# The gate projection of a decoder layer: two of its three split products in one wide matmul

## The chip, the cores and the metric

One core of a Trainium2 chip runs the whole layer as one program. The metric is the device time of one execution in microseconds (us). The kernel before took 356.97 us as the median of 3 executions (356.93 to 357.1). The profile comes from one further execution.

## The reference

The reference is one hybrid decoder layer on 256 tokens of width 1024, all in float32. Cut to what matters here:

```
h    = rmsnorm(x)
proj = h @ w_in               # queries, keys, values of two mixers | g_m (2 x 1024 columns)
gm   = sigmoid(g_m)           # the merge gates
mixed = gm[:, :1024] * (y_nsa @ w_up_nsa) + gm[:, 1024:] * (y_moba @ w_up_moba)
x    = x + mixed @ w_out
x    = x + relu(rmsnorm(x) @ w_ff1)**2 @ w_ff2
return rmsnorm(x)
```

`y_nsa` and `y_moba` are the outputs of two attention mixers. The change lies in the projection to `g_m`, the gates.

## The kernel before

**Split products.** TensorE is given its operands as float32r, and the layer is float32. So every operand is split into a high and a low part: ScalarE (ACT) writes the high part with a Copy (`whi`, line 114), and VectorE (DVE) subtracts it from the number to get the low part (`wlo`, line 116). A product is then three matmuls into the same PSUM columns: high weights with high activations, high weights with low activations, low weights with high activations (`mm3`, line 256). The activations of the gates are split in the same way, into `hTh` and `hTl`.

**Chunks and slots.** The weights come in chunks of 128x2048 numbers (`CHUNKS`, line 24). Each chunk has a slot of the program: its matmuls are a list, and `run_slot` (line 227) issues them in order and puts other work of all engines between them at given fractions of the list (`at(0.1, ...)`). Inside one engine everything runs strictly in the order in which it was issued. In the slot of chunk c, the chunk c+2 is split in halves (`split_events`, line 295) and the chunk c+5 is loaded.

**The gates.** Chunks 12 to 19 are the eight gate groups, here called groups 0 to 7. A group makes two blocks of 128 gates x 256 tokens. Each block sums 8 steps of 128 model columns, with three matmuls of 256 columns in a step: 48 matmuls in a group (`two_blocks` and `wstat`, lines 790 and 285). Both blocks of a group share one PSUM bank, except in group 0, which has a bank for each. The banks go round in the order `acc0`, `tp`, `acc1` (line 819; `next_bank`, line 68). At fraction 0.02 of the next slot `gm_evac` (line 808) takes the bank with one ScalarE Tanh of 512 columns (line 816).

**Attention beside the gates.** The same slots hold the attention, two head pairs at a time (`unit_events`, line 657). In an odd slot (groups 1, 3, 5, 7) TensorE makes the scores `Sa`, `Sb` and the products with the values (`yb`), VectorE masks the scores and finds their maxima (lines 572 to 576), and ScalarE takes the exponentials (line 585). In the even slot after it (groups 2, 4, 6 and the first slot after the gates) VectorE normalizes the probabilities (`d_norm`, lines 590 to 599, at fraction 0.1) and TensorE transposes them (`d_trans`, line 615, at fraction 0.78; for the first pair of them at another place). ScalarE and VectorE then copy the transposes to SBUF (lines 617 and 619).

**After the gates.** Two slots each of `upn` and `upm` multiply the mixers' outputs up and merge them with the gates. Four slots `wout` follow, here called output slots 0 to 3, and then the feed-forward part (FF1, FF2). All of them draw banks from the same round until the first FF1 slot, where line 1156 sets the round anew: `turn["acc"] = ["acc1", "acc0"]`, so that its first block always goes into bank `acc1`. The results of an output slot are added to x by VectorE (line 906), scaled and rounded to high parts by ScalarE (line 910), and VectorE makes the low parts (line 913). Output slot 3 has a bank for each of its two blocks; its second block is added at fraction 0.02 of the first FF1 slot.

Of the kernel before, what the change touches and what calls it, by code (L numbers as in the profile page):

```python
# [9 lines left out]
F32R = mybir.dt.float32r  # L10
AF = mybir.ActivationFunctionType
ALU = mybir.AluOpType
# [33 lines left out]
def hybrid_layer(ctx: ExitStack, tc: tile.TileContext, gxd, w, w1c, small, const, gf, out):  # L46
    nc = tc.nc
    act, dve, pool, pe = nc.scalar, nc.vector, nc.gpsimd, nc.tensor
# [3 lines left out]
    cp = ctx.enter_context(tc.tile_pool(name="cp", bufs=1))  # L52
# [15 lines left out]
    def next_bank(kind):  # L68
        t = turn[kind]
        t.append(t.pop(0))  # L70
        return bank(t[-1], kind)

    def acc_tile():
        return next_bank("acc")
# [13 lines left out]
    raw, hi, lo = {}, {}, {}  # L88
# [87 lines left out]

    def act_tiles(name):
        return [cp.tile([128, 2048 + e], F32R, name=name + n, tag="act" + n.upper())  # L180
                for n, e in (("h", 128), ("l", 16))]

    def act_views(tiles, o):
        return (a[:, o:o + 2048].rearrange("p (k q) -> p k q", k=8) for a in tiles)

    h_tiles = act_tiles("hT")
    hTh, hTl = act_views(h_tiles, 16)
    hNh, hNl = act_views(h_tiles, 0)  # L190

    for kt in range(8):
        act.activation(hTh[:, kt, :], xT[:, kt, :], AF.Copy, scale=g1[:, kt:kt + 1])
# [30 lines left out]
    def at(pos, f, *a):  # L224
        ev.append((pos, f, a))

    def run_slot(mms):
        n = len(mms)
        es = sorted(ev, key=lambda e: e[0])
        ev.clear()  # L230
        j = 0
        for i, m in enumerate(mms):
            while j < len(es) and es[j][0] <= i / n:
                es[j][1](*es[j][2])
                j += 1
            m()
        while j < len(es):
            es[j][1](*es[j][2])
            j += 1

    def paired(v):

        return v.rearrange("p (a b) -> p b a", a=2)
# [5 lines left out]
                           a=2, b=128)  # L249

    def mm(o, l, r, start, stop):
        if len(r.shape) > len(o.shape):
            o = o.rearrange("p (b a) -> p b a", a=2)
        pe.matmul(o, l, r, start=start, stop=stop, skip_group_check=True)  # L254

    def mm3(o, lh, ll, rh, rl, first, last):
        return [lambda: mm(o, lh, rh, first, False),
                lambda: mm(o, lh, rl, False, False),
                lambda: mm(o, ll, rh, False, last)]
# [25 lines left out]
    def wstat(o, c, off, nk, ncol, ah, al, ks=None, first=0, last=None):  # L285

        r = []
        last = nk - 1 if last is None else last
        for k in (range(nk) if ks is None else ks):
            a = k * ncol + off  # L290
            r += mm3(o, hi[c][:, a:a + 128], lo[c][:, a:a + 128], paired(ah[:, k, :]),
                     paired(al[:, k, :]), k == first, k == last)
        return r

    def split_events(c, hs, ls):
# [8 lines left out]
    def std_events(c):  # L304
        if c == C_QM + 1:
            split_events(c, (0.0, 0.51), (0.3, 0.52))
        elif c == C_VM + 1:
            split_events(c, (0.0, 0.06), (0.09, 0.6))
        elif 9 <= c < 20 and c % 2:
            split_events(c, (0.0, 0.06), (0.09, 0.46))  # L310
        elif 9 <= c < 20:
            split_events(c, (0.0, 0.45), (0.3, 0.8 if c > 10 else 0.92))
        else:
            split_events(c, (0.0, 0.45), (0.3, 0.46))
# [342 lines left out]
    def unit_events(s):  # L657
        d = (s - 9) // 2
        if not 9 <= s <= 21:
            return  # L660
        if s % 2 == 0:
            at(0.1, d_norm, d)
            if s != 12:
                at(0.78 if d else 0.9, d_trans, d)
            return
        late = {11: 0.04, 13: 0.22}.get(s, 0)
        if s == 13:
            at(0.06, d_trans, d - 1)
        if d > 0:
            at(0.1 + late, d_cmp, d - 1)  # L670
        if d < 6:
            at(0.1 + late, d_scores, d)
        if d > 0:
            at(0.1 + late, d_pv, d - 1)
        if d < 6:
            at(0.11 + late, d_max, d)
            at(0.2 + late if s > 12 else 0.5, d_exp, d, 1)
            at(0.22 + late if s > 12 else 0.52, d_exp, d, 0)
        if d > 0:
            at(0.12 + late, d_yevac, d - 1)  # L680
# [4 lines left out]
    for sec, c0, n in groups:  # L685
# [6 lines left out]
        for i in range(2):  # L692
            c = c0 + i
# [96 lines left out]
    def two_blocks(c, ah, al, late=8, whole=None):  # L790

        if late < 8:
            outs = [acc_tile()[:, 0:256] for _ in range(2)]
            whole = None
            order = [range(late), range(late, 8)]
        else:
            whole = whole or acc_tile()
            outs = [whole[:, 0:256], whole[:, 256:512]]
            order = [range(8)]
        mms = []  # L800
        for ks in order:
            for m in range(2):
                mms += wstat(outs[m], c, m * 128, 8, 256, ah, al, ks=ks, last=7)
        return mms, outs, whole

    sgs = [ap_.tile([128, 8, 256], F32, name="sga", tag="early")]

    def gm_evac(g, outs, whole):
        if g == 4:
            sgs.append(ap_.tile([128, 8, 256], F32, name="sgb", tag="w1"))  # L810
        v = sgs[g // 4][:, 2 * (g % 4):2 * (g % 4) + 2]
        if whole is None:
            for m in range(2):
                act.activation(v[:, m], outs[m], AF.Tanh, scale=0.5)
        else:
            act.activation(v.rearrange("p b q -> p (b q)"), whole, AF.Tanh, scale=0.5)

    prev = [(evac_tm, ("vm", 1, accs[1], 512))]
    turn["acc"] = ["acc0", "tp", "acc1"]
    for g in range(8):  # L820
        c = C_GM + g
        if g == 0:
            for k in (4, 6):
                at(0.0, norm_parts, k, k + 2)
        std_events(c)
        unit_events(c)
        for f, a in prev:
            at(0.02, f, *a)
        mms, outs, whole = two_blocks(c, hNh, hNl, 8 if g else 4)
        run_slot(mms)  # L830
        prev = [(gm_evac, (g, outs, whole))]

    mxh, mxl = act_views(act_tiles("mx"), 0)

    def up_views(k):
        return [v[:, 2 * k:2 * k + 2].rearrange("p b q -> p (b q)")
# [18 lines left out]
    for sec, c0, kind, evac in (("upn", C_UPN, "n", upn_evac), ("upm", C_UPM, "m", upm_evac)):  # L855
        for i in range(2):
            c = c0 + i
            if c == C_UPN:
                split_events(c, (0.3, 0.3), (0.4, 0.4))
            elif c == C_UPM:  # L860
                split_events(c, (0.0, 0.0), (0.1, 0.53))
            elif c < C_UPM:
                split_events(c, (0.0, 0.0), (0.1, 0.1))
            else:
                split_events(c, (0.0, 0.0), (9, 9))
            unit_events(c)
            for f, a in prev:
                at(0.02, f, *a)
                if f == upm_evac:
                    at(0.15, mix_l, a[0])  # L870
            accs = [acc_tile(), acc_tile()]
            mms = []
            for m in range(4):
                mms += wstat(accs[m // 2][:, m % 2 * 256:m % 2 * 256 + 256], c, m * 128, 4, 512,
                             yTh[kind], yTl[kind])
            at(0.52, evac, 2 * i, accs[0])
            if kind == "m":
                at(0.7, mix_l, 2 * i)
            run_slot(mms)
            prev = [(evac, (2 * i + 1, accs[1]))]  # L880
# [50 lines left out]
    for i in range(4):  # L931
        c = C_WOUT + i
        if i == 0:
            at(0.03, mix_l, 3)
            lo_late(0.35, c - 1)
        elif i == 1:
            lo_late(0.03, c - 1)
        split_events(c, (0.0, 0.1) if i else (0.0, 0.3), ((9, 9), (0.3, 0.3), (0.3, 0.3), (9, 9))[i])
        for f, a in prev:
            at(0.02, f, *a)  # L940
        if i == 1:
            at(0.01, open_ff)
            for j in range(4):
                at(0.9, gamma_rows, j)
        if i == 3:
            outs = [acc_tile()[:, 0:256] for _ in range(2)]
            at(0.52, wout_evac, i, outs, (0,))
            run_slot([m for j in range(2)
                      for m in wstat(outs[j], c, j * 128, 8, 256, mxh, mxl)])
            prev = [(wout_evac, (i, outs, (1,)))]  # L950
        else:
            mms, outs, _ = two_blocks(c, mxh, mxl, 6 if i == 0 else 8)
            run_slot(mms)
            prev = [(wout_evac, (i, outs))]
# [191 lines left out]
    for c in range(C_FF, NCH - 2):  # L1146
        sec, i, _ = CHUNKS[c]
# [5 lines left out]
        prev = []  # L1153
        if sec == "ff1":
# [4 lines left out]
            mms, outs, whole = two_blocks(c, FB["h2h"], FB["h2l"], 8 if i else 6)  # L1159
# [4 lines left out]
            prev = [(squares, (i, outs, whole))]  # L1164
# [17 lines left out]
    whole = ops[order[3]]  # L1182
# [148 lines left out]
```

## Time and profile before

| | |
|---|---|
| median of 3 executions | 356.97 us |
| the profiled execution | 357.63 us |
| its span in the trace | 355.9 us |
| TensorE busy | 347.4 us |
| VectorE busy | 312.9 us |
| ScalarE busy | 242.9 us |
| granted TensorE clock, mean | 0.995 |

The span runs from the first to the last instruction in the trace; the profiled execution's own time lies 1.7 us above it. A row of the timeline reads: start and duration in us, engine, line, operation, output and inputs, count, and in square brackets the idle time of the engine ahead of it and what ended that. A row of the chain reads: start, duration, engine, what it writes, line and count. Matmuls are pipelined: a row's duration is a latency, and the distance of starts is the pace.

### The profile page before, as it was taken

The page shows a single profiled execution, that of the slowest core. Times are in us where ns is not written, and L with a number is a line of the kernel's source. Part 1 is how long each engine was busy: PE and PEld are TensorE (multiplying, and loading weights), DVE is VectorE, ACT ScalarE, POOL GpSimd, SP SyncE. Part 2 cuts the span into 40 slices and gives each one's busy share as a digit, 9 for nine tenths or more (in the row PEclk, how much of TensorE's full clock was granted, in tenths as well). Part 3 has the DMA queues.
Part 4 walks back from the last instruction along what each step waited for, and adds up shares of the span by engine and source line. Part 5 has one row for each costly group of instructions (what it writes and reads, how often), then busy time and mean ns, then how long its engine had stood idle before and what let it go on. Part 6 is the DMA issues. An engine that isn't in the chain of part 4 may idle for free.

```text
span 355.9 us, 6587 instructions
## 1 busy us (share of the span) xinstructions
PE 347.4 (98%) x2667; PEld 324.4 (91%) x2667; DVE 312.9 (88%) x456; ACT 242.9 (68%) x367; POOL 25.9 (7%) x46
## 2 busy tenths in 40 slices
PE   7999999999999999999999999999999999999993
PEld 5997888889999999999999999999999999999982
DVE  4988999999876859767968999999999999999794
ACT  5974965879646757625448799877777769676713
POOL 1010000000000000000312011110111111000001
PEclk9999999999999999999999999999999999999997
DMA  7987535434443333633697957888889888774003
GB/s 263 389 335 283 193 120 192 161 120 126 159 174 135 120 120 131 225 120 118 171 330 227 346 163 273 297 260 258 263 281 289 278 268 301 196 308 170 1 2 118
DMA packets 14447, 73.69 MB, mean 207 GB/s; under 512 B 1744, under 2 KB 3152, under 8 KB 7120
## 3 DMA queue, kind: packets, MB, share of 16 engines
q1 hardware_dynamic: 10512, 64.68, 50.4%
q0 software_dynamic: 3328, 7.87, 9.5%
q10 hardware_dynamic: 576, 0.72, 0.6%
q8 instruction: 21, 0.34, 0.4%
q14 instruction: 10, 0.08, 0.1%
HBM read 72.21 MB, written 1.05 MB: 206 GB/s over the span
## 4 chain that ended last, share of the span: by engine, by line
PE 90%; DVE 3%; ACT 2%; DMA 1%; issue 1%; SPq 0%; POOLq 0%; POOL 0%; DVEq 0%
PE acc L254 61%; PE o L254 10%; PE yb L254 5%; PE tp L254 3%; PE kvbacc L254 3%; PE qacc L254 2%; PE Sa L254 2%; PE Sa L615 2%; DMA gx<-in_gx_dram 1%; PE tp L354 1%; PE Sb L615 1%; DVE x L1066 1%; PE Sb L254 1%; PE o L927 0%; ACT whi L114 0%
## 5 line engine op out<-in xcount | busy, mean ns | idle before, releaser
L114 ACT ACTIVATE whi<-raw 128x1024 fp32r<-128x1024 f32 (+3 forms) x82 | 90.1, 1120 | 43.1 <-DMA raw<-in_ff_dram 26.7
L116 DVE TENSOR_TENSOR wlo<-raw,whi 128x1024 fp32r<-128x1024 f32 (+3 forms) x83 | 105.0, 1285 | 5.3 <-ACT whi L114 4.8
L254 PE MATMUL acc<-h2h,whi 128*128 128x256 f32 x256 | 70.5, 275 | 0.0
L254 PE MATMUL acc<-h2h,wlo 128*128 128x256 f32 x256 | 70.4, 275 | 0.0
L254 PE MATMUL acc<-h2l,whi 128*128 128x256 f32 x256 | 70.4, 275 | 0.0
L254 PEld LDWEIGHTS acc<-h2l,whi 128*128 128x128 f32 x256 | 49.2, 192 | 0.0
L254 PEld LDWEIGHTS acc<-h2h,wlo 128*128 128x128 f32 x256 | 49.2, 192 | 0.0
L254 PEld LDWEIGHTS acc<-h2h,whi 128*128 128x128 f32 x256 | 49.2, 192 | 0.0
L254 PE MATMUL acc<-hTh,wlo 128*128 128x256 f32 x128 | 35.8, 279 | 0.0
L254 PE MATMUL acc<-hTl,whi 128*128 128x256 f32 x128 | 35.4, 277 | 0.0
L254 PE MATMUL acc<-hTh,whi 128*128 128x256 f32 x128 | 35.3, 276 | 0.0
L1037 ACT ACTIVATE whi<-wt 128x2048 fp32r<-128x2048 f32 x14 | 26.7, 1907 | 9.4 <-PE acc L254 7.4
L1039 DVE TENSOR_TENSOR wlo<-wt,whi 128x2048 fp32r<-128x2048 f32 x14 | 32.0, 2284 | 0.2
L254 PEld LDWEIGHTS acc<-hTh,wlo 128*128 128x128 f32 x128 | 24.5, 192 | 0.5 <-issue 0.5
L254 PEld LDWEIGHTS acc<-hTl,whi 128*128 128x128 f32 x128 | 24.6, 192 | 0.2 <-issue 0.2
L254 PE MATMUL acc<-whi,hTh 128*128 128x512 f32 (+2 forms) x65 | 24.1, 371 | 0.5 <-ACT whi L114 0.4
L254 PEld LDWEIGHTS acc<-hTh,whi 128*128 128x128 f32 x128 | 24.6, 192 | 0.0
L1030 DVE TENSOR_TENSOR sl<-raw,sh 128x1536 fp32r<-128x1536 f32 x14 | 24.5, 1748 | 0.0
L254 PE MATMUL acc<-wlo,hTh 128*128 128x512 f32 (+2 forms) x65 | 24.1, 371 | 0.3 <-DVE wlo L116 0.2
L254 PE MATMUL acc<-whi,hTl 128*128 128x512 f32 (+2 forms) x65 | 23.8, 366 | 0.0
L1028 ACT ACTIVATE sh<-raw 128x1536 fp32r<-128x1536 f32 x14 | 20.8, 1488 | 0.0
L1021 POOL DMA_DIRECT2D wt<-in_ff_dram x14 | 12.3, 880 | 89.5 <-DMA wt<-in_ff_dram 89.5
(322 smaller groups left out, 891.1 us busy)
## 6 DMA issues: line engine op xcount, KB each, us to landing
raw<-in_ff_dram SPq DMA_DIRECT2D x32, 1024.0 KB, 7.7
raw<-in_gm_dram SPq DMA_DIRECT2D x8, 1024.0 KB, 4.8
wt<-in_ff_dram POOLq DMA_DIRECT2D x28, 256.0 KB, 7.4
raw<-in_wout_dram SPq DMA_DIRECT2D x4, 1024.0 KB, 4.8
raw<-in_q_dram SPq DMA_DIRECT2D x2, 1024.0 KB, 6.7
raw<-in_qm_dram SPq DMA_DIRECT2D x2, 1024.0 KB, 6.4
raw<-in_km_dram SPq DMA_DIRECT2D x2, 1024.0 KB, 5.6
raw<-in_vm_dram SPq DMA_DIRECT2D x2, 1024.0 KB, 4.8
```

The costliest lines, as they stand in the source:

```text
L114: act.activation(hi[c][:, a:b], raw[c][:, a:b], AF.Copy)
L116: dve.tensor_tensor(lo[c][:, a:b], raw[c][:, a:b], hi[c][:, a:b].bitcast(F32), op=ALU.subtract)
L254: pe.matmul(o, l, r, start=start, stop=stop, skip_group_check=True)
L354: pe.transpose(tp[:, j * 256 + t * 128:j * 256 + t * 128 + 128], src[:, t, (2 * i + j) * 128:(2 * i + j + 1) * 128], ident)
L615: pe.transpose(T[:, j, x, o:o + 128], P[:, 2 * x + j, c:c + 128], ident)
L1021: pool.dma_start(T[:, 1], w["ff2"][i, :, 0:512], accum_op=ALU.add)
L1028: act.activation(singles[c][0], v, AF.Copy)
L1030: dve.tensor_tensor(singles[c][1], v, singles[c][0].bitcast(F32), op=ALU.subtract)
L1037: act.activation(hi[c], v, AF.Copy)
L1039: dve.tensor_tensor(lo[c], v, hi[c].bitcast(F32), op=ALU.subtract)
L1066: dve.scalar_tensor_tensor(x1[:, t, s], y, fst[:, 4 + t:5 + t], x1[:, t, s], op0=ALU.mult, op1=ALU.add)
```

## The change

High and low activations are now one tile `hT` of 2 x 8 x 256 numbers, so that one matmul can read both: `wstat2` multiplies the high weights with the high and the low activations of a step in one product of 512 columns. It writes two halves of a whole bank: columns 0 to 255 hold high x high, columns 256 to 511 high x low. The low weights with the high activations add to the first half with a matmul of 256 columns. A step has two matmuls where it had three, and a group 32 where it had 48.

So each block needs a bank of its own, and the two halves are still to be added: `gm_sum` copies the second half to SBUF on ScalarE and VectorE adds the first half from PSUM to it; `gm_tanh` is a further ScalarE instruction on the sum. Of a group's first block the sum stands at fraction 0.52 of its own slot, of the second block at 0.02 of the next slot, and the Tanh half a slot later than the sum. The diff, cut to its core:

```
-        return [cp.tile([128, 2048 + e], F32R, name=name + n, tag="act" + n.upper())
-                for n, e in (("h", 128), ("l", 16))]
+        return cp.tile([128, 2, 8, 256], F32R, name=name, tag="act")
...
+    def wstat2(o, c, off, nk, ncol, a, ks=None):
+        r = []
+        for k in (range(nk) if ks is None else ks):
+            w = slice(k * ncol + off, k * ncol + off + 128)
+            both = a[:, :, k, :].rearrange("p x (a b) -> p x b a", a=2)
+            m = [lambda w=w, both=both, k=k: mm(o, hi[c][:, w], both, k == 0, k == nk - 1),
+                 lambda w=w, k=k: mm(o[:, 0:256], lo[c][:, w], paired(a[:, 0, k, :]), False, False)]
+            r += m if k < nk - 1 else m[::-1]
+        return r
...
-            act.activation(v.rearrange("p b q -> p (b q)"), whole, AF.Tanh, scale=0.5)
+        act.activation(gate(g, m), o[:, 256:512], AF.Copy)
+        dve.tensor_tensor(gate(g, m), o[:, 0:256], gate(g, m), op=ALU.add)
+
+    def gm_tanh(g, m):
+        act.activation(gate(g, m), gate(g, m), AF.Tanh, scale=0.5)
...
-        mms, outs, whole = two_blocks(c, hNh, hNl, 8 if g else 4)
-        run_slot(mms)
-        prev = [(gm_evac, (g, outs, whole))]
+        if g == 1:
+            at(0.53, gm_tanh, 0, 0)
+        if g:
+            at(0.53, gm_tanh, g - 1, 1)
+        outs = [acc_tile() for _ in range(2)]
+        prev = [(gm_sum, (g, 1, outs[1]))]
+        if g:
+            at(0.52, gm_sum, g, 0, outs[0])
+            prev.append((gm_tanh, (g, 0)))
+        else:
+            prev = [(gm_sum, (g, 0, outs[0]))] + prev
+        run_slot([f for ks in ([range(8)] if g else [range(4), range(4, 8)]) for m in range(2)
+                  for f in wstat2(outs[m], c, m * 128, 8, 256, hT, ks)])
+    prev.append((gm_tanh, (7, 1)))
```

The gates drew 9 banks from the round before (two in group 0, then one a group) and draw 16 now. 9 is a multiple of the three banks and 16 is not: every later slot gets the bank that stands one place further. In output slot 3 the two blocks had `acc0` and `tp` before and have `tp` and `acc1` now.

On VectorE, this is the order before around the end of group 3 and the start of group 4. Lines 572 to 576 are the mask and maxima of group 3's scores, line 116 writes low weights, and lines 590 to 599 are the normalizing in group 4's slot:

```order
L572 TENSOR_TENSOR Sa<-Sa,kc 128x4x128
L575 TENSOR_REDUCE ust<-Sa 128x2x2
L576 TENSOR_SCALAR ust<-ust 128x4
L572 TENSOR_TENSOR Sb<-Sb,kc 128x2x256
L575 TENSOR_REDUCE ust<-Sb 128x2x2
L576 TENSOR_SCALAR ust<-ust 128x4
L655 TENSOR_TENSOR yTln<-yb,yThn 128x256
L116 TENSOR_TENSOR wlo<-raw,whi 128x1024
L590 TENSOR_SCALAR ust<-ust 128x8
L591 RECIPROCAL ust<-ust 128x8
```

The same place now (the lines have moved by 10; line 825 is the new sum):

```order
L116 TENSOR_TENSOR wlo<-raw,whi 128x1024
L825 TENSOR_TENSOR sga<-acc,sga 128x256
L116 TENSOR_TENSOR wlo<-raw,whi 128x1024
L582 TENSOR_TENSOR Sa<-Sa,kc 128x4x128
L585 TENSOR_REDUCE ust<-Sa 128x2x2
L586 TENSOR_SCALAR ust<-ust 128x4
L582 TENSOR_TENSOR Sb<-Sb,kc 128x2x256
L585 TENSOR_REDUCE ust<-Sb 128x2x2
L586 TENSOR_SCALAR ust<-ust 128x4
L665 TENSOR_TENSOR yTln<-yb,yThn 128x256
L116 TENSOR_TENSOR wlo<-raw,whi 128x1024
L825 TENSOR_TENSOR sga<-acc,sga 128x256 x2
```

Two sums, of both blocks of group 3, stand ahead of the normalizing, and the sum of group 2's second block stands ahead of the low weights at the top and so of the mask of group 3's scores.

On ScalarE, before, from the exponentials of group 3 to the copy of group 4's transposes:

```order
L585 ACTIVATE P,ust<-Sa,ust 128x256 x4
L585 ACTIVATE P,ust<-Sb,ust 128x128 x4
L114 ACTIVATE whi<-raw 128x1024
L816 ACTIVATE sga<-acc 128x512
L114 ACTIVATE whi<-raw 128x1024
L617 ACTIVATE PT<-Sa 128x2x2x256
```

and now (line 824 copies a half bank, line 828 is the Tanh):

```order
L595 ACTIVATE P,ust<-Sa,ust 128x256 x4
L595 ACTIVATE P,ust<-Sb,ust 128x128 x4
L824 ACTIVATE sga<-acc 128x256
L828 ACTIVATE sga<-sga 128x256
L114 ACTIVATE whi<-raw 128x1024
L824 ACTIVATE sga<-acc 128x256
L828 ACTIVATE sga<-sga 128x256
L114 ACTIVATE whi<-raw 128x1024
L824 ACTIVATE sgb<-acc 128x256
L828 ACTIVATE sga<-sga 128x256
L627 ACTIVATE PT<-Sa 128x2x2x256
```

The copy for the second sum stands behind the first copy, a Tanh and half a chunk of high weights.

On TensorE, the last products of output slot 3 and the first of the first FF1 slot, before (the numbers tell tiles apart: `acc_2209` is the second block of output slot 3, `acc_2280` the first of FF1):

```order
L254 MATMUL acc_2209<-mxh_1713,whi_2059 128x256
L254 MATMUL acc_2209<-mxl_1714,whi_2059 128x256
L254 MATMUL acc_2209<-mxh_1713,wlo_2060 128x256
L254 MATMUL acc_2280<-h2h_2072,whi_2146 128x256 [waits PE_49,DVE_49,Activation_49,Pool_49]
L254 MATMUL acc_2280<-h2l_2073,whi_2146 128x256
```

and now (`acc_2125` is the second block of output slot 3, `acc_2196` the first of FF1):

```order
L252 MATMUL acc_2125<-mx_1627,wlo_1976 128x256
L252 MATMUL acc_2125<-mx_1627,whi_1975 128x256 x2
L252 MATMUL acc_2125<-mx_1627,wlo_1976 128x256
L252 MATMUL acc_2196<-h2h_1988,whi_2062 128x256 [waits DVE_49,Activation_49,Pool_49]
L252 MATMUL acc_2196<-h2l_1989,whi_2062 128x256
```

The matmuls are the same; what the wait on VectorE counts to is another instruction. `acc_2280` took bank `acc1`, which output slot 2 had used last, and its wait ends with the adds of output slot 2. `acc_2196` takes bank `acc1` too, which now holds the block before it, `acc_2125`, and its wait ends with the add of that block.

More of the change, by code (lines that the diff above doesn't have):

```diff
@@ L172, in hybrid_layer, with act_tile @@
     cmpm = kc_[:, K_CMP:K_CMP + 30].rearrange("p (t i) -> p t i", t=2)
-    def act_tiles(name):
-        return [cp.tile([128, 2048 + e], F32R, name=name + n, tag="act" + n.upper())
-                for n, e in (("h", 128), ("l", 16))]
[L183 to L190, printed above, removed]
+    def act_tile(name):
+        return cp.tile([128, 2, 8, 256], F32R, name=name, tag="act")
+    hT = act_tile("hT")
+    hTh, hTl = hT[:, 0], hT[:, 1]
+    hNh, hNl = hTh, hTl
     for kt in range(8):
@@ L251, in mm @@
     def mm(o, l, r, start, stop):
-        if len(r.shape) > len(o.shape):
+        if len(r.shape) == 4:
+            o = o.rearrange("p (x b a) -> p x b a", x=2, a=2)
+        elif len(r.shape) > len(o.shape):
             o = o.rearrange("p (b a) -> p b a", a=2)
@@ L806, in hybrid_layer, with gate, gm_sum @@
     sgs = [ap_.tile([128, 8, 256], F32, name="sga", tag="early")]
-    def gm_evac(g, outs, whole):
-        if g == 4:
+    def gate(g, m):
+        return sgs[g // 4][:, 2 * (g % 4) + m]
+    def gm_sum(g, m, o):
+        if g == 4 and m == 0:
             sgs.append(ap_.tile([128, 8, 256], F32, name="sgb", tag="w1"))
[L811 to L816, printed above, removed]
+        act.activation(gate(g, m), o[:, 256:512], AF.Copy)
+        dve.tensor_tensor(gate(g, m), o[:, 0:256], gate(g, m), op=ALU.add)
+    def gm_tanh(g, m):
+        act.activation(gate(g, m), gate(g, m), AF.Tanh, scale=0.5)
     prev = [(evac_tm, ("vm", 1, accs[1], 512))]
@@ L828, in hybrid_layer @@
             at(0.02, f, *a)
-        mms, outs, whole = two_blocks(c, hNh, hNl, 8 if g else 4)
-        run_slot(mms)
-        prev = [(gm_evac, (g, outs, whole))]
-    mxh, mxl = act_views(act_tiles("mx"), 0)
+        if g == 1:
[12 more added lines that the diff above has]
+    prev.append((gm_tanh, (7, 1)))
+    mx = act_tile("mx")
+    mxh, mxl = mx[:, 0], mx[:, 1]
     def up_views(k):
```

## The prediction

> **What bounds the kernel now.** I read the page first, for the shares of the engines and of the chain:
>
> ```profile
> PE 347.4 (98%) x2667; PEld 324.4 (91%) x2667; DVE 312.9 (88%) x456; ACT 242.9 (68%) x367; POOL 25.9 (7%) x46
> PE 90%; DVE 3%; ACT 2%; DMA 1%; issue 1%; SPq 0%; POOLq 0%; POOL 0%; DVEq 0%
> ```
>
> TensorE is busy for 98% of the span. A saving shows only if it shortens TensorE's own stream, and a wait of TensorE anywhere is lost in full. VectorE (88%) is close behind and can be late. Then I read the chain of waits in order of time (start, us, engine, what, line, count):
>
> ```profile
> 91.72 8.01 PE acc L254 x70
> 99.73 0.87 PE Sa L615 x8
> ...
> 105.77 9.24 PE acc L254 x81
> 115.01 0.87 PE Sa L615 x8
> ...
> 121.34 9.24 PE acc L254 x81
> 130.58 0.87 PE Sa L615 x8
> ...
> 210.32 5.36 PE acc L254 x48
> 215.68 2.59 PE o L254 x12
> ```
>
> From 91.7 us on the chain is TensorE without a break: the gates, then the transposes of groups 2, 4 and 6 (line 615), and so on to the end of FF2. The last two rows give the paces. 48 products of 256 columns take 5.36 us, 111.7 ns each; 12 of 512 columns take 2.59 us, 215.8 ns each.
>
> **The change part by part. TensorE's pace.** A step had three products of 256 columns, 3 x 111.7 = 335.0 ns. Now it has one of 512 and one of 256: 215.8 + 111.7 = 327.5 ns. The columns are the same 768; 7.5 ns of spacing go. There are 8 groups x 2 blocks x 8 steps = 128 steps: a gain of 128 x 7.5 ns = 1.0 us. From below: if two halves at a distance cost extra, nothing is gained. From above: if the 256-column product, now beside a longer one, drops to half of a 512 (107.9 ns), each step saves 11.3 ns, 1.4 us in all. I take 1.0, the sum of measured paces.
>
> [...]
>
> **The evacuation and the three transposes.** Each block now costs ScalarE a copy and a Tanh and VectorE a sum, all of 256 columns. These rows stand nearest (timeline of group 1's slot, then a 512-column Tanh and the row behind it):
>
> ```profile
> 91.77 0.38 ACT L654 ACTIVATE yThn<-yb 128x256 fp32r<-128x256 f32 x1 [2.85 <-PE yb L254]
> 93.64 0.42 DVE L655 TENSOR_TENSOR yTln<-yb,yThn 128x256 fp32r<-128x256 f32 x1
> 93.97 1.21 DVE L116 TENSOR_TENSOR wlo<-raw,whi 128x1024 fp32r<-128x1024 f32 x1
> ...
> 111.66 0.59 ACT L816 ACTIVATE sga<-acc 128x512 f32<-128x512 f32 x1
> 112.13 1.06 ACT L114 ACTIVATE whi<-raw 128x1024 fp32r<-128x1024 f32 x1
> ```
>
> A ScalarE instruction is done after 0.38 us, and at 512 columns the next starts after 0.47, so I estimate a spacing of 0.25 at 256. A sum on VectorE takes 0.42, with 0.33 to the next. What counts is where they queue. In groups 2, 4 and 6 TensorE transposes probabilities that VectorE normalizes first. Now the two sums of the group before stand ahead of the normalizing, and the second of them needs a copy that stands on ScalarE behind a copy, a Tanh (two in group 1) and half a chunk of high weights. Group 4 on VectorE and ScalarE, before:
>
> ```profile
> 103.18 1.23 DVE L116 TENSOR_TENSOR wlo<-raw,whi 128x1024 fp32r<-128x1024 f32 x1 [0.28 <-ACT whi L114]
> 104.32 0.69 DVE L572 TENSOR_TENSOR Sa<-Sa,kc 128x512 f32<-128x512 f32 x1
> 109.93 0.17 DVE L590 TENSOR_SCALAR ust<-ust 128x8 f32<-128x8 f32 x1 [0.46 <-ACT P L585]
> 110.64 1.83 DVE L599 TENSOR_TENSOR P<-P,ust 128x512 f32<-128x512 f32 x2
> 116.36 0.69 DVE L619 COPY PT<-Sb 128x512 f32<-128x512 f32 x1 [2.76 <-PE Sb L615]
> 106.57 0.47 ACT L585 ACTIVATE P<-Sa,ust 128x256 f32<-128x256 f32 x1 [0.37 <-DVE ust L576]
> 109.66 0.24 ACT L585 ACTIVATION_READ_ACCUMULATOR P<-Sb,ust 128x1 f32 x1
> 110.69 1.07 ACT L114 ACTIVATE whi<-raw 128x1024 fp32r<-128x1024 f32 x1 [0.80 <-PE acc L254]
> ```
>
> The normalizing ran from 109.93 to 110.64 + 1.83 = 112.47, 2.54 us, and the transposes began at 115.01: 2.5 us of cover. Now, on the same clock: the exponentials (done 109.90) follow the mask on VectorE (`[0.37 <-DVE ust L576]`), and the mask is pushed back by the sum of group 2's second block. That sum waits for ScalarE's high weights and copy: I estimate 0.78 us. So ScalarE is free at about 110.55; a copy and a Tanh (0.5), half a chunk (0.97, from 110.69 to 111.66 above), the copy (0.38): 112.4. The sum: 112.8. The normalizing: 115.35. TensorE, quicker by 26 steps x 7.5 ns = 0.2, is there at 114.8. It waits 0.55 us.
>
> The same for groups 2 and 6:
>
> ```profile
> 95.47 1.09 ACT L114 ACTIVATE whi<-raw 128x1024 fp32r<-128x1024 f32 x1
> 95.65 0.17 DVE L590 TENSOR_SCALAR ust<-ust 128x8 f32<-128x8 f32 x1 [0.46 <-ACT P L585]
> 96.36 1.83 DVE L599 TENSOR_TENSOR P<-P,ust 128x512 f32<-128x512 f32 x2
> 125.49 0.17 DVE L590 TENSOR_SCALAR ust<-ust 128x8 f32<-128x8 f32 x1 [0.47 <-ACT P L585]
> 125.93 1.83 DVE L599 TENSOR_TENSOR P<-P,ust 128x512 f32<-128x512 f32 x2
> ```
>
> Group 2: the transposes began at 99.73, only 1.5 us behind the normalizing (98.19). ScalarE free at 95.47 + 0.2 (group 0's two sums, less VectorE's idle there), then 3 x 0.25, 0.97, 0.38, the sum 0.42 and 2.54: 100.7, against 99.55. A wait of 1.2 us. Group 6: ScalarE free at 125.4 + 0.45 (the mask there waited for TensorE's scores, which takes up part), 0.5, 0.97, 0.38, 0.42, and 2.27 to normalize (125.49 to 127.76): 130.4, against 130.58 - 0.2 = 130.4. No wait. Together 1.8 us. Bounds: none if the delays are half of these; 3.3 if each is 0.5 us longer.
>
> **The bank of the first FF1 block.** The round of banks ends one place further, so FF1's first block goes into the bank that the last block of output slot 3 has just filled, and waits for VectorE's add of it. Before, TensorE went on, while VectorE was late there:
>
> ```profile
> 187.49 0.28 PE L254 MATMUL acc<-h2h,whi 128*128 128x256 f32 x1
> 187.94 0.41 DVE L906 TENSOR_TENSOR gx<-gx,acc 128x256 f32<-128x256 f32 x1
> 188.93 0.48 DVE L913 SCALAR_TENSOR_TENSOR h2l<-gx,h2h 128x256 fp32r<-128x256 f32 x1 [0.58 <-ACT h2h L910]
> 189.33 0.41 DVE L906 TENSOR_TENSOR gx<-gx,acc 128x256 f32<-128x256 f32 x1
> ...
> 181.59 1.06 ACT L114 ACTIVATE whi<-raw 128x1024 fp32r<-128x1024 f32 x1 [6.69 <-DMA raw<-in_ff_dram]
> 183.07 0.88 DVE L913 SCALAR_TENSOR_TENSOR h2l<-gx,h2h 128x256 fp32r<-128x256 f32 x2 [3.41 <-ACT h2h L910]
> ```
>
> FF1's first product started at 187.49. The add of the last block (the second of the two rows of line 906) ran to 189.33 + 0.41 = 189.74. The new wait is 2.3 us with the signal. VectorE was late because ScalarE had stood 6.69 us for FF1's first chunk, which came at 181.59; that load follows work of the output slots, so it moves with TensorE and the distance stays. Bounds: 0.5 if VectorE is on time (an add and its signal), 2.8 if it is later by 0.5. Nothing takes it back: TensorE has no idle time left to fill.
>
> **At nothing.** The one tile for `hTh` and `hTl` shifts what lies behind it by 576 bytes; products of 256 columns take 275 ns on every pair of tiles (70.5 us / 256 for `h2h`, as for `hTh`), so the place in SBUF does not show. The first gate product now also waits for the low activations, 0.1 us at most, one product earlier than before. Banks come round inside the gates in time: group 3's first block is summed at about 111.35 (copy 0.38, sum 0.42 from 110.55), and its bank is next filled by group 4's second block, four steps and a wide product ahead of 114.8, at 113.3. The Tanh are hidden by ScalarE's wait for the transposes; with that cover gone each would cost 0.25 us. Loads move with the splits, by less than their lead.
>
> **Sum.** -1.0 + 1.8 + 2.3 = +3.1 us. The span goes from 355.9 to 359.0 and the profiled execution from 357.63 to 360.7; on the median of 356.97 it is 360.1 us, slower by 0.9%. A difference under 0.2% (0.7 us) can't be told from none here.
>
> **Rivals.** First, only the bank costs: the gates' sums fit into the cover, as group 6 nearly does. For it: ScalarE is idle for 0.80 us before group 4's weights, and my delays are estimates of 0.1 us precision in a chain of ten. Against it: group 2 has the least cover. -1.0 + 2.3 = +1.3: 358.3 us, chance 0.16.
>
> Second, not slower: transfers come early. The place is the arrival of FF1's first chunk. If held-up gates let it land 1.8 us earlier against TensorE, VectorE's add is on time and the wait falls to 0.5. With the gates at their lower bound and the pace at its upper: -1.4 + 0 + 0.5 = -0.9: 356.1 us. Before, the chunk came 5.9 us ahead of FF1's first product (181.59 to 187.49); from about 7.7 us on the add is in time. Against it: the load is issued behind VectorE's low weights, which stand behind the merge. Chance 0.05; without its full size, no change, 0.04.
>
> Third, the clock falls: a still TensorE gets a lower granted clock.
>
> ```profile
> PEclk9999999999999999999999999999999999999997
> L156 PE MATMUL yb<-ident 128*128 128x128 f32 x14 | 3.1, 409 | 1.4 <-POOL ones L157 1.4
> L615 PE MATMUL Sa<-ident,P 128*128 128x128 f32 x48 | 6.3, 275 | 0.0
> ```
>
> A transpose took 409 ns in the warm-up at the start and 275 later, so a slow state exists. If the 2.3 us bring it back for a stretch as long as the warm-up (3.1 us), at (409 - 275) / 409 of it, 1.0 us is lost, and at half pace up to 1.6: 361.1 to 361.7 with the rest. [...] Chance 0.08.
>
> **How the numbers follow.** My case has 0.67; its own range is 358.6 (gates 0.3) to 361.6 (gates 3.3). With the first rival's 358.3 and the longer waits (gates 3.3, bank 2.8: 362.1) the range is 358.1 to 362.2. Slower: 0.67 + 0.16 + 0.08 = 0.91; no change 0.04; faster 0.05.
>
> **What would show it.** In the changed profile, products of the gates at 215.8 and 111.7 ns; idle time of TensorE of 1.2 and 0.55 us before line 625 (the transposes) in groups 2 and 4, ended by VectorE's line 609; one wait of 2.3 us at FF1's first product, ended by line 930. I am wrong if TensorE shows no idle time at FF1, if the gates' steps come faster than 320 ns, or if the idle time lies elsewhere.

## The result, and the profile after

The changed kernel takes 359.63 us (median of 5 runs, 359.10 to 360.71) against 356.97 for the kernel before: a ratio of 1.0086, 95% interval 1.0073 to 1.0098. The profiled execution took 360.71 us, with a span of 358.9; before it was 357.63 and 355.9. So the span grew by 3.0 us, where the sum of the prediction had 3.1. That the two are so near is partly luck: in this execution the stages that the change touches grew by 3.5 us, and the rest was 0.5 us shorter.

The page, first the busy times, then the chain by engine:

```profile
PE 346.6 (97%) x2539; PEld 320.0 (89%) x2539; DVE 318.4 (89%) x472; ACT 249.0 (69%) x390; POOL 25.9 (7%) x46
PE 76%; DVE 10%; ACT 7%; DMA 4%; issue 2%; SPq 0%; POOLq 0%; POOL 0%; DVEq 0%; ACTq 0%
```

TensorE has 128 products less and is busy 0.8 us less. But the chain, which was TensorE's for 90%, now runs through VectorE, ScalarE and a DMA for 21%. Which products of TensorE wait (waits of TensorE: total us, times, longest us); before had neither row:

```profile
PE acc L252 <- DVE gx L930: 1.9, 1, 1.9
PE Sa L625 <- DVE P L609: 1.8, 2, 1.2
```

Where the time went, by stages: the gates, then the merge and the output slots, then FF1 to the end (start:end, length, busy time of each engine, granted clock, DMA share, GB/s). Of the kernel before:

```profile
79.80:141.40 61.60, 61.60 (x580) 58.39 (x579) 49.78 (x78) 41.46 (x109) 0.00 (x0) 1.00 0.39 138
141.40:187.49 46.09, 46.09 (x416) 45.50 (x415) 34.24 (x49) 22.82 (x29) 4.19 (x7) 1.00 0.58 190
187.49:355.90 168.41, 162.13 (x1178) 153.77 (x1176) 159.19 (x179) 121.17 (x117) 19.34 (x27) 0.99 0.69 227
```

and of the changed kernel:

```profile
79.56:142.70 63.14, 61.24 (x450) 53.77 (x451) 53.78 (x88) 45.21 (x126) 0.00 (x0) 1.00 0.38 134
142.70:190.76 48.06, 46.15 (x415) 45.40 (x414) 36.88 (x58) 25.57 (x37) 5.12 (x9) 1.00 0.58 193
190.76:358.90 168.14, 161.93 (x1176) 153.92 (x1176) 157.84 (x174) 120.23 (x114) 18.46 (x26) 0.99 0.70 224
```

The gates grew by 1.54 us, the stage up to FF1 by 1.97. The start and the rest, which the change does not touch, are 0.24 and 0.27 shorter; executions of one kernel differ by as much (five of the kernel before took from 356.6 to 357.1 us).

The chain of the changed kernel in order of time (start, us, what), first group 2 and then the way to FF1:

```profile
95.58 0.61 ACT sga L828 x2
96.19 0.95 ACT whi L114
97.14 0.28 ACT sga L824
97.45 0.42 DVE sga L825
98.50 1.84 DVE P L609 x2
100.38 1.09 PE Sa L625 x8
...
173.86 8.51 DMA raw<-in_ff_dram
182.45 1.06 ACT whi L114
...
190.28 0.34 DVE gx L930
190.76 2.25 PE acc L252 x18
```

The upper rows are the queue that the prediction described: two Tanh, half a chunk of high weights, the copy, the second sum, the normalizing, and only then the transposes. The lower rows are the other term: FF1's first chunk is 8.5 us on its way, ScalarE takes it at 182.45, and the row of output work behind it ends with the add on VectorE for which FF1's first product waits.

### The profile page after: what moved, and what is told of

It is laid out like the page before. It is cut to its first block, busy times and chain, and to the rows that moved or that the text cites. A ratio compares the mean times of both kernels' runs of the same rounds, so it can differ in the third digit from the quotient of the medians.

```text
span 358.9 us, 6365 instructions
## 1 busy us (share of the span) xinstructions
PE 346.6 (97%) x2539; PEld 320.0 (89%) x2539; DVE 318.4 (89%) x472; ACT 249.0 (69%) x390; POOL 25.9 (7%) x46
## 4 chain that ended last, share of the span: by engine, by line
PE 76%; DVE 10%; ACT 7%; DMA 4%; issue 2%; SPq 0%; POOLq 0%; POOL 0%; DVEq 0%; ACTq 0%
PE acc L252 48%; PE o L252 9%; PE yb L252 4%; PE tp L252 3%; PE qacc L252 3%; PE kvbacc L252 2%; DVE wlo L116 2%; DMA raw<-in_ff_dram 2%; ACT whi L114 2%; ACT P L595 2%; DMA gx<-in_gx_dram 1%; PE Sa L625 1%; PE Sa L252 1%; PE tp L364 1%; DVE P L609 1%
## 5 line engine op out<-in xcount | busy, mean ns | idle before, releaser
L252 PE MATMUL acc<-hT,whi 128*128 128x512 f32 x128 | 42.1, 385 | 0.1
L252 PE MATMUL acc<-whi,hT 128*128 128x512 f32 (+2 forms) x130 | 38.4, 370 | 0.6 <-ACT whi L114 0.6
L252 PE MATMUL acc<-hT,wlo 128*128 128x256 f32 x128 | 32.7, 276 | 0.0
L252 PEld LDWEIGHTS acc<-whi,hT 128*128 128x128 f32 x130 | 24.1, 190 | 4.0 <-ACT whi L114 0.9
L252 PEld LDWEIGHTS acc<-hT,whi 128*128 128x128 f32 x128 | 23.1, 190 | 3.1 <-issue 0.8
L252 PEld LDWEIGHTS acc<-hT,wlo 128*128 128x128 f32 x128 | 24.5, 191 | 1.0 <-issue 0.2
L252 PE MATMUL acc<-wlo,hT 128*128 128x512 f32 (+2 forms) x65 | 24.1, 371 | 0.2 <-DVE wlo L116 0.2
L252 PE MATMUL acc<-mx,whi 128*128 128x256 f32 x128 | 21.5, 275 | 0.0
L252 PEld LDWEIGHTS acc<-mx,whi 128*128 128x128 f32 x128 | 19.4, 192 | 0.0
```

## The experiments

Medians are given over the median of the kernel before on the same chip: 356.80 us beside the first four kernels, 356.89 beside the next four, 357.00 beside the last four. The ratios and their intervals come from the same runs, but are not the ratios of these medians.

**The bank undone.** In the changed kernel:

```diff
-                turn["acc"] = ["acc1", "acc0"]
+                turn["acc"] = ["acc0", "acc1"]
```

> The changed kernel with the round of banks begun at FF1 one place on, so that FF1's first block takes the bank that output slot 3's first block left, as before the change, and only FF1's second block takes the bank of output slot 3's last block. My theory (the bank costs what TensorE's 1.92 us at FF1's first product show): that wait goes, the second block starts about 2.0 us later than the first and the add is done by then, so 1.7 to 2.0 us less than the changed kernel, 357.4 to 357.9 us; the waits at the transposes of groups 2 and 4 stay at 1.2 and 0.6 us. Rival (the bank is not what is late there, but VectorE's and ScalarE's whole queue, and TensorE meets it one product on): the wait moves to FF1's second block or to the next operand, and the time stays within 0.5 us of the changed kernel's, 359.1 to 359.9 us.

358.61 us, 1.81 over before (ratio 1.0064, interval 1.0048 to 1.0080). TensorE's last output product and FF1's first, then ScalarE's high weights of FF1's first chunk:

```profile
188.57 0.28 PE L252 MATMUL acc<-mx,wlo 128*128 128x256 f32 x1
188.68 0.28 PE L252 MATMUL acc<-h2h,whi 128*128 128x256 f32 x1
180.89 1.06 ACT L114 ACTIVATE whi<-raw 128x1024 fp32r<-128x1024 f32 x1 [4.82 <-DMA raw<-in_ff_dram]
```

The wait is gone and did not come back at the second block; the waits at the transposes stayed at 1.2 and 0.6 us. So the bank is the cause of the wait. (FF1's first block took `acc0` here, which output slot 2 had used last, not the bank of output slot 3's first block.) But the time fell by 0.9 us only (2.66 to 1.81 over before), not by 1.7 to 2.0, and that difference is not clear of the scatter: the interval of the changed kernel's ratio beside the next four is 1.0046 to 1.0082. What the wait was worth in the median is so not shown by this pair. The last row shows why it may be little: here the same chunk arrived 1.56 us earlier than in the trace of the changed kernel, with all else in front of it at the same time to 0.01 us.

**The second sum behind the normalizing.** In the changed kernel:

```diff
-            at(0.02, f, *a)
+            at(0.12 if g % 2 == 0 and f == gm_sum else 0.02, f, *a)
```

> The changed kernel with the sum of the second block put, in the slots of groups 2, 4 and 6 whose transposes wait, behind the normalizing of the probabilities on VectorE (from 0.02 to 0.12 of the slot); nothing is left out. My theory (the waits at the transposes come from the order of the queue, with the second sum behind half a chunk of high weights ahead of the normalizing): the idle 1.24 and 0.57 us before the transposes of groups 2 and 4 go, 1.6 to 2.1 us less than the changed kernel, 357.3 to 357.9 us; the 1.9 us at FF1 stay. Rival (it is the added work of ScalarE and VectorE, two copies, two sums and a second Tanh for each group, wherever it stands): at most half of the idle time goes, 358.7 to 359.6 us.

357.40 us, 0.60 over before (1.0020, 1.0003 to 1.0037). VectorE in group 2, and its add at FF1:

```profile
97.61 1.83 DVE L609 TENSOR_TENSOR P<-P,ust 128x512 f32<-128x512 f32 x2
99.36 0.42 DVE L825 TENSOR_TENSOR sga<-acc,sga 128x256 f32<-128x256 f32 x1
...
187.45 0.42 DVE L930 TENSOR_TENSOR gx<-gx,acc 128x256 f32<-128x256 f32 x1 [0.34 <-PE acc L252]
```

The edit moves the sum and, with it, ScalarE's copy for it, since `gm_sum` issues both. The sum now runs behind the normalizing, and no transpose waits any more (those of groups 2, 4 and 6 start at 99.93, 114.99 and 130.31 with no idle time shown ahead of them): the order was the cause, not the work, all of which is still there. The last row is unlooked for. The add waits for TensorE's product, so VectorE is on time, and TensorE's wait at FF1 is 0.60 us instead of 1.92. In this execution ScalarE took the chunk at 179.29, 7.96 us ahead of the time at which TensorE was ready.

**Both.** The two edits together.

> The changed kernel with both edits: FF1's banks as before the change, and the second block's sum behind the normalizing in groups 2, 4 and 6. My theory (three terms that add: pace -1.0, waits at the transposes +1.8, bank +1.9 to +2.3): only the pace is left, 355.6 to 356.2 us, faster than both the kernel before and the changed one. Rival (pace gains are lost elsewhere, or one wait takes the place of the other when it is removed): 356.8 us or more, no faster than the kernel before.

> The kernel with both edits once more, on one chip with the kernel whose gate products are taken apart, so that the two can be held against each other: 356.0 to 356.6 us, 0.5 us less than the kernel before.

356.26 us, 0.54 under before (0.9984, 0.9974 to 0.9995), and 356.20 the second time, 0.80 under (0.9981, 0.9972 to 0.9989). This version beats both kernels; 356.26 lies just above the range expected. The waits of TensorE in the body are gone, and the gates take (second execution)

```profile
79.64:140.25 60.61, 60.54 (x450) 53.78 (x450) 53.46 (x88) 45.33 (x126) 0.00 (x0) 1.00 0.38 139
```

60.61 us, 0.99 less than before and 2.53 less than in the changed kernel.

**The bank alone, in the kernel before.** Ahead of output slot 3:

```diff
+            turn["acc"] = ["acc0", "acc1"]
```

> The kernel before the change, with nothing but its round of banks shifted at output slot 3, so that FF1's first block takes the bank of that slot's last block, as in the changed kernel. My theory (the bank alone makes the wait at FF1): TensorE waits 2.0 to 2.3 us there for VectorE's add, 358.9 to 359.3 us. Rival (the wait in the changed kernel needs the gates' delays, which push VectorE and ScalarE back): no more than 0.5 us, 356.9 to 357.5 us.

358.78 us, 1.98 over before (1.0064, 1.0043 to 1.0085), just under the range expected, its six runs from 357.67 to 360.28. So the wait needs none of the gates' delays. Its profiled execution took 358.26 us, and showed the chunk early and VectorE waiting for TensorE (ScalarE, VectorE, TensorE):

```profile
179.36 1.06 ACT L114 ACTIVATE whi<-raw 128x1024 fp32r<-128x1024 f32 x1 [4.76 <-DMA raw<-in_ff_dram]
187.76 0.42 DVE L906 TENSOR_TENSOR gx<-gx,acc 128x256 f32<-128x256 f32 x1 [0.57 <-PE acc L254]
188.33 0.35 PE L254 MATMUL acc<-h2h,whi 128*128 128x256 f32 x1 [0.61 <-DVE gx L906]
```

The median speaks for the theory and the trace shows the small wait. Both are so if the wait differs from execution to execution with the landing. No kernel here has two traces with different landings, so that this happens within one kernel is argued; between kernels the table further down shows it.

**The changed kernel again.**

> The changed kernel once more, on the same chip as the three next to it. My theory (the wait at FF1's first product is set by when FF1's first chunk of weights lands, which differs from execution to execution): if the chunk lands 7.0 us after its issue, as in the trace of the bank experiment, the wait is about 0.9 us and the time about 359.3 us; if it lands 8.6 us after it, as in the first trace of the changed kernel, the wait is 1.9 us and the time about 360.5 us; the waits at the transposes are 1.2 and 0.6 us either way. Rival (the wait is of one size and the spread comes from the start of the kernel): 1.9 us with either landing.

359.55 us, 2.66 over before (1.0064, 1.0046 to 1.0082), seven runs from 358.90 to 362.31; the profiled one was the slowest. Its chunk was issued at 173.81 and taken at 182.43, 8.62 us later, and the wait was 1.95 us, as expected for a late landing. The 360.5 us expected with it were wrong: 362.31. TensorE behind the wait:

```profile
190.75 0.35 PE L252 MATMUL acc<-h2h,whi 128*128 128x256 f32 x1 [1.95 <-DVE gx L930]
...
191.82 0.28 PE L252 MATMUL acc<-h2h,whi 128*128 128x256 f32 x1
191.94 0.31 PE L252 MATMUL acc<-h2l,whi 128*128 128x256 f32 x1
192.05 0.42 PE L252 MATMUL acc<-h2h,wlo 128*128 128x256 f32 x1
...
195.45 0.28 PE L252 MATMUL acc<-h2h,whi 128*128 128x256 f32 x1
```

1.3 us after TensorE went on, a product takes 0.42 us instead of 0.28, and from 192.05 to 195.45 there are 16 spacings of 213 ns instead of 111.7: 1.6 us lost. The stretches of this execution show the granted clock (the number behind the busy times):

```profile
193.00:194.00 1.00, 1.00 (x7) 1.00 (x7) 1.00 (x2) 0.00 (x0) 0.00 (x0) 0.50 0.60 178
195.00:196.00 1.00, 1.00 (x9) 1.00 (x8) 1.00 (x1) 0.00 (x0) 0.15 (x1) 0.77 0.83 123
```

It is half. In the first trace of the changed kernel, after a wait of 1.92 us, it stayed at 1.00. That is the prediction's third rival, in one execution and not in the other.

FF1's first chunk in the traces (us; "ready" is the start of TensorE's last output product and one spacing of 0.11):

| kernel | issued | ScalarE takes it | later by | ready | ahead of ready | TensorE idle at FF1 |
|---|---|---|---|---|---|---|
| changed | 173.86 | 182.45 | 8.59 | 188.68 | 6.2 | 1.92 |
| changed, again | 173.81 | 182.43 | 8.62 | 188.63 | 6.2 | 1.95 |
| second block's copy on VectorE | 172.18 | 179.54 | 7.36 | 186.99 | 7.5 | 1.17 |
| second sum moved | 172.43 | 179.29 | 6.86 | 187.25 | 8.0 | 0.60 |
| before, bank alone | 172.38 | 179.36 | 6.98 | 187.56 | 8.2 | 0.61 |

The earlier the chunk stands ahead of TensorE, the shorter the wait, down to 0.6 us: an add of 0.42 us (the row at 187.45 above, for the 0.60) and what lies between its end and TensorE's start. The time from issue to landing differs between executions by up to 1.8 us (6.86 to 8.62 in the table, 8.64 in a trace below), and no edit changes that load itself; the cause of the difference stays open.

**The pace taken back.** In the kernel with both edits, each product of 512 columns as two of 256:

```diff
-            m = [lambda w=w, both=both, k=k: mm(o, hi[c][:, w], both, k == 0, k == nk - 1),
+            m = [lambda w=w, k=k, x=x: mm(o[:, 256 * x:256 * x + 256], hi[c][:, w],
+                                          paired(a[:, x, k, :]), k == 0, k == nk - 1)
+                 for x in range(2)]
+            m += [
```

> The kernel with both edits, but with the product of 512 columns of every gate step taken apart into two of 256 columns, into the same two halves of the bank; the sums and their order stay. This prices the pace alone. My theory (335.0 against 327.5 ns for each of 128 steps): 1.0 us more than the kernel with both edits, 357.1 to 357.5 us, no faster than the kernel before, and the gates take 61.6 us instead of 60.6. [...]

357.00 us, 0.11 over before (1.0001, 0.9991 to 1.0012), just under the range expected. Both products of the first step carried the bank's start mark here, and the output is off by a relative 0.38, which I put down to the first one's term of that step being left out of the sum. With the mark on the first of the two alone (`k == 0 and x == 0`), on one chip with the kernel with both edits:

> The kernel with both edits and with the wide product of every gate step taken apart, as before, but with only the first of the two products marked as the bank's start, so that no term is lost. My theory (128 steps of 7.5 ns): 0.7 to 1.0 us more than the kernel with both edits on the same chip, and the gates take 61.6 to 61.7 us. [...]

357.03 us against 356.20: 0.83 more, and level with the kernel before (0.9998, 0.9989 to 1.0008). The gates:

```profile
79.51:141.21 61.70, 61.59 (x580) 58.37 (x579) 53.70 (x89) 45.74 (x129) 0.00 (x0) 1.00 0.39 137
```

1.09 us more than the 60.61 of the kernel with both edits. The pace term stands: 1.09 us over the 128 steps are 8.5 ns for a step, where the sum of the paces had 7.5.

**FF1's chunk behind the output work.** In the changed kernel, in output slot 2:

```diff
-        split_events(c, (0.0, 0.1) if i else (0.0, 0.3), ((9, 9), (0.3, 0.3), (0.3, 0.3), (9, 9))[i])
+        split_events(c, ((0.0, 0.3), (0.0, 0.1), (0.03, 0.1), (0.0, 0.1))[i], ((9, 9), (0.3, 0.3), (0.3, 0.3), (9, 9))[i])
```

> The changed kernel with one edit: in output slot 2, ScalarE's high weights of the first half of FF1's first chunk come behind the copies of the last output block instead of ahead of them, so that ScalarE does not stand at that chunk with output work queued behind it; FF1's banks stay as changed. My theory (VectorE's add is late because ScalarE waits for that chunk's landing): the wait at FF1's first product falls to 0.5 to 0.7 us whenever the chunk lands, 0.4 to 1.3 us less than the changed kernel, 358.3 to 359.2 us. Rival (VectorE's own queue makes the add late): the wait stays at 0.9 to 1.9 us and the time with it, or FF1's first product waits for its high weights instead.

359.30 us, 2.41 over before (1.0064, 1.0047 to 1.0080): 0.25 less than the changed kernel, less than the 0.4 expected. TensorE's wait is 0.77 us, although the chunk came late in this trace (issued at 173.55, taken at 182.19, 8.64 us later): with a landing like this the changed kernel waited 1.92 and 1.95 us. So the add is late because output work stands on ScalarE behind the chunk. The six runs lie between 359.14 and 359.90, those of the changed kernel between 358.90 and 362.31. That the median moves little because most executions of the changed kernel had short waits is likely, but no trace of them shows it.

**The second block's copy on VectorE.** In the changed kernel:

```diff
-        act.activation(gate(g, m), o[:, 256:512], AF.Copy)
+        if m:
+            dve.tensor_copy(gate(g, m), o[:, 256:512])
+        else:
+            act.activation(gate(g, m), o[:, 256:512], AF.Copy)
```

> The changed kernel with one edit: the copy of the second block of each gate group is VectorE's, not ScalarE's, so that the second sum no longer waits for half a chunk of high weights; the order of the queues stays, and VectorE gets 8 copies of about 0.35 us more. My theory (most of the wait at the transposes is the second sum's wait for ScalarE, 1.40 us in group 2 and 1.10 us in group 4): the normalizing comes 1.0 and 0.8 us earlier, idle time of at most 0.4 us is left before group 2's transposes and none before group 4's, 1.7 to 2.2 us less than the changed kernel, 357.4 to 358.1 us. Rival (VectorE is the bound there, so its added 0.35 us for each group cost as much as the wait): no more than 1.0 us less, 358.6 us or more.

358.21 us, 1.32 over before (1.0039, 1.0024 to 1.0053), 1.34 less than the changed kernel: between the two theories. The second sum in group 2 of the changed kernel:

```profile
97.45 0.42 DVE L825 TENSOR_TENSOR sga<-acc,sga 128x256 f32<-128x256 f32 x1 [1.40 <-ACT sga L824]
```

VectorE there in this kernel, and TensorE's transposes:

```profile
95.83 0.42 DVE L828 TENSOR_TENSOR sga<-acc,sga 128x256 f32<-128x256 f32 x1 [0.74 <-ACT sga L827]
96.17 0.41 DVE L825 COPY sga<-acc 128x256 f32<-128x256 f32 x1
96.62 0.42 DVE L828 TENSOR_TENSOR sga<-acc,sga 128x256 f32<-128x256 f32 x1
96.96 0.16 DVE L600 TENSOR_SCALAR ust<-ust 128x8 f32<-128x8 f32 x1
...
99.54 0.66 PE L625 MATMUL Sa<-ident,P 128*128 128x128 f32 x4 [0.75 <-DVE P L609]
```

The second sum's wait of 1.40 us is gone and a copy of 0.45 stands in its place. But 0.75 us of TensorE's wait is left, not 0.4: the first sum's wait of 0.74 stays, and that sum starts at 95.83 where the changed kernel has it at 95.62, though the gates here began 0.2 us earlier (79.33 against 79.56): VectorE's queue ahead of it is longer. The starts of the transposes, read as in the next section, show 1.5 us gone of the 2.5 that groups 2, 4 and 6 lost, but in group 2 only 0.6 of 1.4. So half a chunk of high weights ahead of the copy is the larger part. What is left is not taken apart further, since the edit itself adds copies to VectorE's queue: the mask ahead of group 2 starts 0.45 us later against the start of the gates.

**The pause made longer.** In the changed kernel, ahead of the add that FF1's first product waits for, one scratch sum of 128x1024, then two:

```diff
+        for _ in range(1 if i == 3 and ms == (1,) else 0):
+            v = xT[:, 0:4].rearrange("p k q -> p (k q)")
+            dve.tensor_tensor(FB["scr"], v, v, op=ALU.add)
```

> The changed kernel with one sum of 128x1024 into a scratch tile (1.2 us on VectorE) put ahead of the add that FF1's first product waits for, so that TensorE's pause there grows from 0.9 to 2.0 us to 2.1 to 3.2 us; the scratch sum is used by nothing. In one of two traces of the changed kernel, TensorE's granted clock was halved for 3.4 us, 1.2 us after a pause of 1.95 us, and cost 1.6 us; in the other, after 1.92 us, it was not. My theory (a longer pause makes the halved clock likelier, and it comes in some executions and not in others at this length): times in two groups, 360.6 to 361.0 us without it and 362.0 to 362.6 us with it, some of each. Rival (the halved clock has nothing to do with the pause): 1.2 us more than the changed kernel, 360.7 us, in nearly all executions.

> As the kernel with one scratch sum, but with two, so that the pause at FF1 is 3.3 to 4.4 us. My theory: the halved clock comes in nearly every execution, with products of 256 columns at 213 ns for 3 to 3.4 us behind the pause: 2.4 + 1.6 us more than the changed kernel, 363.2 to 364.0 us. Rival (the halved clock has nothing to do with the pause): 2.4 us more, 361.7 to 362.2 us, and products at 111.7 ns behind the pause.

With one sum the six runs are 359.87, 360.05 and 360.63, and 362.70, 362.73 and 363.53: two groups, as the theory had it, but the lower one reaches 0.7 us under what was expected and the upper one 0.9 over it. The mean granted clock was 0.995 to 0.997 in the first group and 0.993 to 0.994 in the second. The profiled execution was of the first, with a pause of 1.73 us and the clock at 1.00 behind it. With two sums the median is 363.11, just under the range expected; five of the six runs took 362.68 to 366.12 us at a mean clock of 0.991 to 0.993, and one took 361.06 at 0.998. Why one took 366.12 is open. TensorE's first FF1 product in the profiled one, and a stretch 0.6 us later:

```profile
192.38 0.35 PE L252 MATMUL acc<-h2h,whi 128*128 128x256 f32 x1 [3.66 <-DVE gx L933]
193.00:194.00 1.00, 1.00 (x7) 1.00 (x6) 1.00 (x2) 1.00 (x1) 0.00 (x0) 0.50 1.00 166
```

The halved clock came behind the pauses of 1.95 and 3.66 us and not behind those of 1.73 and 1.92, and by the groups of times it comes oftener with a longer one: in three of the six runs with one sum and in five of the six with two. For the executions without a trace that is argued from their time and mean clock, not shown. The mean clock is a weak sign: it counts the end of the program too, where TensorE's products are over and the clock falls. In the first trace of the changed kernel, with a mean of 0.996, the only halved stretch is that end: 1.00 from 4.7 to 356.1 us, 0.50 from 356.2 on.

## Why the prediction was right, and where it was off

**Pace, -1.0 us: right.** The steps run as summed (TensorE in the gates of the changed kernel):

```profile
97.78 0.38 PE L252 MATMUL acc<-hT,whi 128*128 128x512 f32 x1
98.00 0.27 PE L252 MATMUL acc<-hT,wlo 128*128 128x256 f32 x1
98.11 0.38 PE L252 MATMUL acc<-hT,whi 128*128 128x512 f32 x1
```

0.33 us for a step, against 0.335 before. The gates without waits take 60.61 us instead of 61.60, and taking the pace back cost 1.09 in the stage and 0.83 in the median.

**The transposes, +1.8 us: the mechanism right, the term too small.** It is 2.5 us: 63.14 in the gates of the changed kernel less 60.61. In medians it is 2.35 (bank undone less both edits) or 2.06 (changed less second sum moved); the last holds a difference of the waits at FF1 as well. The step that failed is "Together 1.8 us", with "No wait" for group 6, and in it the time at which TensorE comes to the transposes. I took 99.73, 115.01 and 130.58 from the rows of the chain, which begin at the modelled end of the product before. The transposes started 0.16 us earlier, at 99.57, 114.85 and 130.42. The row of group 4, before:

```profile
114.85 1.04 PE L615 MATMUL Sa<-ident,P 128*128 128x128 f32 x8
```

In group 4 I also counted only 0.65 of the 0.78 us by which I had ScalarE held up (109.90 to 110.55). With both put right the same working gives 1.3, 0.8 and 0.2 us, 2.3 in all: the queues were sized well, and TensorE was there sooner. The waits that the view shows, 1.24 and 0.57 us, look like the 1.2 and 0.55 forecast, but the view counts from the modelled end of the last product (0.28 us after its start at 256 columns, 0.38 at 512), while the next would have started after 0.11 or 0.22: it leaves out 0.16 to 0.17 us of each stop. The distance of the starts shows all of it. The transposes of groups 0, 4 and 6 in the changed kernel (group 2 at 100.38, above), and of groups 0, 2, 4 and 6 in the kernel with both edits:

```profile
85.20 1.06 PE L625 MATMUL Sa<-ident,P 128*128 128x128 f32 x8
116.22 1.09 PE L625 MATMUL Sa<-ident,P 128*128 128x128 f32 x8 [0.57 <-DVE P L609]
131.80 1.09 PE L625 MATMUL Sa<-ident,P 128*128 128x128 f32 x8
```

```profile
85.34 1.07 PE L625 MATMUL Sa<-ident,P 128*128 128x128 f32 x8
99.11 1.04 PE L625 MATMUL Sa<-ident,P 128*128 128x128 f32 x8
114.15 1.04 PE L625 MATMUL Sa<-ident,P 128*128 128x128 f32 x8
129.47 1.04 PE L625 MATMUL Sa<-ident,P 128*128 128x128 f32 x8
```

From each to the next it is 15.18, 15.84 and 15.58 us against 13.77, 15.04 and 15.32: 1.41, 0.80 and 0.26 us lost in groups 2, 4 and 6. Group 6 was late by so little that no idle time is shown at all.

**The bank, +2.3 us: the mechanism right, the size that of a late landing.** In the first trace it is 190.76 - 188.68 = 2.1 us. In medians it is 0.85 (changed less bank undone), 1.14 (second sum moved less both edits) and 1.98 (bank alone less before). The step that failed is "that load follows work of the output slots, so it moves with TensorE and the distance stays". The issue does keep its distance from TensorE: 187.49 - 172.68 = 14.81 us before, 188.68 - 173.86 = 14.82 after. The landing does not: it came 8.9 us after the issue in the trace from which I worked, 8.6 in the first of the changed kernel, and about 7 in others. One trace gave one draw of it. The bounds of 0.5 to 2.8 held what came, 0.6 to 2.1; the value should have been put nearer the middle.

**The sum.** -1.0 + 2.5 + 2.1 = 3.6 us of the first trace, of which the start and the rest took back 0.5. In medians -0.8 + 2.35 + 0.85 = 2.4, against 2.66 measured. A term too large by about 1.4 and one too small by 0.5 to 0.7 gave 360.1 where 359.6 came.

**The rivals.** The first (only the bank costs) is out: with the bank undone 1.81 us are left. The second named the right quantity, the chunk's arrival ahead of FF1, and a point of 7.7 us from which the add is in time: at 7.5 us the wait was 1.17, at 8.0 it was at its floor. But landing early saves only part, and the gates' loss stays. The third (the clock falls) happens, in two of the four traced executions with a pause of 1.7 us or more, at the price of 1.6 us at half pace that I had worked out; as a part of the likeliest case, and not instead of it. The transposes of 409 ns at the start, from which I argued for it, do not show it by themselves: the view of stretches of the kernel before has the granted clock at 1.00 from 0 to 4 us, where they stand.

**The first FF1 product, the transposes, the Tanh.** The other steps held: the Tanh cost TensorE nothing (with all of them in it, the gates of the kernel with both edits take 60.61 us, the 61.60 of before less the pace), and the waits were where the prediction put them.

## What to carry to other kernels

Saved time on the bound engine is worth its sum only if the operations that pay for it do not stand ahead of work that this engine waits for: here 1.0 us of pace cost 2.5 us, and moving the paying operation 0.1 of a slot gave all of that back. When a change draws a different number of buffers from a round, follow the round to the next place where a buffer is taken just after it was filled. A term that rests on the landing of a transfer has the spread of the landings (6.9 to 8.9 us here), so take it from several executions. And read a stop of TensorE, and the time at which it would be somewhere, from the starts of its products, not from the idle time shown or from the rows of the chain.

## What the runs showed of the hardware

The granted clock was halved for 3.4 us from 1.3 us after a pause of 1.95 us in one execution, and not after 1.92 us in another of the same kernel. With one scratch sum it stayed at 1.00 after a pause of 1.73 us; with two it was halved for 3.4 us from 0.6 us after a pause of 3.66 us (0.97 from 192 to 193 us, 0.50 to 196, 0.83 from 196 to 197). Each is a single execution, and the pauses are counted from modelled ends of products. From what length of pause on the clock falls, and what sets the 1.3 and 0.6 us, is not shown.

The first chunk of FF1 took 6.9 to 8.9 us from issue to ScalarE (6.86 with the second sum moved, 8.91 in the kernel before: issued at 172.68, taken at 181.59), in programs that are alike around it. What sets that stays open.
